# Transposes and value products of an attention stage in batches of two key block pairs, with the output transposes moved to another PSUM bank

## The chip, the cores and the metric

The kernel runs on one core of one Trainium2 chip. The metric is the device time of one execution in microseconds (us). The engines are TensorE (PE in the profile, with its weight loads as PEld), VectorE (DVE), ScalarE (ACT), GpSimd (POOL) and SyncE (SP, which only issues transfers here). TensorE writes to PSUM, which has eight banks of 128 partitions by 2 KB. The kernel is written in a tile framework: the code says what is computed on which engine, and a scheduler decides, when the program is built, in which order each engine gets its instructions; each engine then executes its list strictly in that order and waits on semaphores.

## The reference

Two layers on 2048 rows of 1024 features in float32. The first (a state space scan beside a convolution) is not touched. The second is sparse attention: an indexer scores all keys, each query keeps its best 256, and 16 heads (four per key head, 64 channels each) attend to the kept ones. Cut to what matters here:

```python
score = jnp.where((key_chunk <= c)[None, None, :], score, -jnp.inf)
_, idx = lax.top_k(score, ksel)                    # ksel = 256
...
logits = jnp.einsum("bqhgd,bqkhd->bqhgk", qb, kg) * scale
p = jax.nn.softmax(logits, axis=-1)
ob = jnp.einsum("bqhgk,bqkhd->bqhgd", p, vg)
...
out = (out * jax.nn.silu(z)) @ w_out
```

## The kernel before

The kernel does not gather keys. It finds each query's threshold by a binary search over the score's bits, writes an additive mask of 0 or a large negative number, and attends densely to all admissible keys with that mask.

**The attention stage.** Queries come in 16 tiles of 128 rows, in the order `ORDER = (3, 7, 4, 6, 5, 8, 2, 9, 1, 10, 11, 12, 0, 13, 14, 15)`. Tile i has `nb = i + 1` key blocks of 128 keys. A tile has four units (two pairs of key heads `kp` times two pairs of query heads `hp`), so there are 64 units; a unit has two key heads `e` and two query heads `h` of each. A unit goes through two functions:

- `weights` multiplies the stacked queries `qs` with the keys (`ps_s`, line 1117, two parts `kh` and `kl`); DVE adds the mask and finds the maximum (`lm` and `mx`, line 1121); ACT takes the exponential of `lm` in place (line 1132).
- `values` transposes the weights `lm` block by block on PE (`ps_pt`, line 1148, four 128x128 transposes for one pair of key blocks of one `e`, a "group"); a copy brings the group from PSUM to SBUF (`pT`, line 1153 on ACT; line 1151 on DVE for every other group of the two longest tiles); PE multiplies it with the values `v` (`ps_pv`, line 1155, two matmuls per group, each of which stands as two records in the trace). At the unit's end ACT copies the sum (`ov`, line 1159), PE transposes it back (`ps_ot`, line 1163, four transposes), and DVE multiplies it with the gate (`zt_a` and `avt`, line 62).

The loop emits `weights` of a unit, then `values` of the unit before, so the scheduler can fill gaps of the one with work of the other. The query stacks of the next two units (`ps_q`, line 772, copied by ACT as `qs`, line 774) come in between.

**PSUM in this stage.** `ps_s` has two buffers of two banks (`pq`). Pool `pt2` has three banks, which `ps_pt` and `ps_q` take in turn. Pool `pv` has one bank, which `ps_pv` and `ps_ot` share.

**The selection beside it.** The masks of tiles 12 to 15 are made during this stage by a generator (`select_mask`) that advances one step per 800 mask columns. A tile needs 34 counting passes over its scores. Tile 13 counts on ACT (line 994: a sign pass, then two instructions of one column each, lines 1002 and 1004); tiles 12, 14 and 15 count on DVE (line 977, with two small POOL instructions, line 69, between counts). Their buffers exist once, so tile 14 starts when tile 13 has finished, and tile 15 after 14. A mask must be complete before its tile's units.

Of the kernel before, what the change touches and what calls it, by code (L numbers as in the profile page):

```python
# [11 lines left out]
F32 = mybir.dt.float32  # L12
# [11 lines left out]
P = 128  # L24
# [18 lines left out]
class Tags:  # L43


    def __init__(self, *turns):
        self.turns, self.n = turns, {}
# [839 lines left out]
def index_scores(k, i, S, st, ip, tk, pi, identr, res):  # L887
# [10 lines left out]
    if res is not None:  # L898
        sc = res["sc"] = tk.tile([P, LATE * P], F32, tag="sc", name="sc", bufs=CHAINS + 1)
    split = res is not None  # L900
# [33 lines left out]
def all_mask(k, i, ip, width, mask_d):  # L934

    nc = k.nc
    nk = (i + 1) * P
    eq = ip.tile([P, width], BF16, tag="eq", name="eq", bufs=CHAINS)[:, 0:nk]
    nc.gpsimd.memset(eq, 0.0)
# [118 lines left out]
class Attend:  # L1058
# [3 lines left out]
    def __init__(self, k, S, kvt, pools, ident, identr, beside, pace):  # L1062
        self.k, self.S, self.kvt, self.ident, self.identr = k, S, kvt, ident, identr
        self.am, self.tm, self.qsp, self.ap, self.pp, self.ptp, self.pq, self.pt, self.pv_ = pools
        self.beside, self.pace, self.cols = beside, pace, 0
        self.masks = {}

    def load(self, i, kp):

# [66 lines left out]
    def values(self, t, hp, prob):  # L1136

        k, nc, ap_, ident = self.k, self.k.nc, self.ap, self.ident
        nb, kp = t["i"] + 1, t["kp"]
        np_ = P if nb > 1 else 64  # L1140
        po = self.pv_.tile([P, 2, 256], F32, tag="pv", name="ps_pv")
        for e in range(2):
            for b in range(0, nb, 2):
                n = min(2, nb - b)
                ps = self.pt.tile([P, 2, 2, 128], F32, tag="pt", name="ps_pt")
                for s in range(n):
                    for h in range(2):
                        nc.tensor.transpose(ps[:, s, h], prob[e][h][:, (b + s) * P:(b + s + 1) * P], ident)  # L1148
                pT = self.ptp.tile([P, 2, 256], F32, tag="pT", name="pT")
                if b % 4 == 2 and nb > 14:  # L1150
                    nc.vector.tensor_copy(pT[:, 0:n], ps[:, 0:n].rearrange("p s h q -> p s (h q)"))
                else:
                    nc.scalar.copy(pT[:, 0:n], ps[:, 0:n].rearrange("p s h q -> p s (h q)"))  # L1153
                for s in range(n):
                    nc.tensor.matmul(po[64 * s:64 * s + 64, e],  # L1155
                                     self.kvt[(b + s) // 8, kp][2][:, (b + s) % 8, e * 64:e * 64 + 64], pT[:, s],
                                     start=b == 0, stop=b + s >= nb - 2)
        ov = ap_.tile([P, 2, 256], F32, tag="ov", name="ov", bufs=2)
        nc.scalar.copy(ov[0:np_], po[0:np_])
        ps = self.pv_.tile([P, 2, 2, 128], F32, tag="pv", name="ps_ot")  # L1160
        for e in range(2):
            for h in range(2):
                nc.tensor.transpose(ps[:, e, h, 0:np_], ov[0:np_, e, h * P:h * P + P], ident[0:np_, 0:np_])  # L1163
        four = t["z"].rearrange("p (e g h c) -> p g e h c", e=2, g=2, h=2)[:, hp]
        rd = ap_.tile([P, 2, 2], F32, tag="rd", name="rd", bufs=4)
        nc.vector.reciprocal(rd, t["den"].rearrange("p (e g h) -> p g e h", e=2, g=2)[:, hp])
        zr = ap_.tile([P, 2, 2, 64], F32, tag="zr", name="zr", bufs=2)
        k.vtt(zr, four, rd[:, :, :, None].to_broadcast([P, 2, 2, 64]), ALU.mult, nc.gpsimd)
        k.vtt(four, ps[:, :, :, 0:64], zr, ALU.mult)
        if nb > 1:  # L1170
            u = ap_.tile([P, 2, 2, 64], F32, tag="avt", name="avt", bufs=2)
            k.vtt(u, ps[:, :, :, 64:128], zr, ALU.mult)
            k.vtt(four, four, u, ALU.add, nc.gpsimd)
        if hp == 1:
            nc.sync.dma_start(self.S["att"][t["rows"], 512 * t["kp"]:512 * t["kp"] + 512], t["z"])
# [2 lines left out]
ORDER = (3, 7, 4, 6, 5, 8, 2, 9, 1, 10, 11, 12, 0, 13, 14, 15)  # L1178
RATIO = 2
CHAINS = 3  # L1180
ON_ACT = (3, 5, 7, 9, 11, 13)
EARLY = 140
PACE = 800
# [4 lines left out]
def layer1(k, A, h1_d, S, ident, identr, vec):  # L1188
    nc, tc = k.nc, k.tc
    with ExitStack() as ctx:  # L1190
# [3 lines left out]
        with ExitStack() as c2:  # L1194
# [21 lines left out]
            def index(tiles):  # L1216

                todo, scoring, running, turn = list(tiles), None, [], 0
                while todo or scoring or running:
                    if scoring is None and todo and len(running) <= CHAINS:  # L1220
                        i = todo.pop(0)
# [5 lines left out]
                    if scoring and (not running or turn % RATIO == 0):  # L1227
                        if next(scoring[0], scoring) is scoring:
                            res, scoring = scoring[1], None
                            if res is not None:  # L1230
                                running.append(select_mask(k, res["i"], res["sc"], tk, LATE * P, CHAINS, S["mask"],
                                                       scalar=res["i"] in ON_ACT))
                    turn += 1
# [46 lines left out]
            def late():  # L1280
                for j in range(LATE, 16):
                    sc = tk.tile([P, L], F32, tag="sc", name="scr")
                    nc.sync.dma_start(sc[:, 0:(j + 1) * P], S["sc"][j, :, 0:(j + 1) * P])
                    yield from select_mask(k, j, sc, tk, L, 1, S["mask"], pace, scalar=j in ON_ACT)
                    done.add(j)
# [199 lines left out]
```

## Time and profile before

| what | value |
|---|---|
| median of 3 runs | 3014.05 us (3012.71 to 3017.12) |
| profiled execution | 3015.91 us, span 3014.1 us |
| mean granted clock of TensorE | 0.969 |
| attention stage in the trace | about 1799 to 2817 us of the span |
| transposes of the weights / value products | 2176 records each |
| after the stage (output projection) | 2817 to 3014 us |

A row of a group in the profile names line, engine, operation, what is written and read, count, then busy time and mean duration (ns), then the idle time of the engine just before. A row of the stretches gives, for each engine, the time in which it was busy, with the number of instructions, then the granted clock, the share of the transfer engines and GB/s. A row of the timeline gives start and duration in us, and how many instructions of one kind followed each other.

### The profile page before, as it was taken

To read this page: it belongs to the slowest core of one execution; us is meant where nothing else is said; L and a number is where in the kernel's file an instruction comes from. 1 tells how busy PE (TensorE), PEld (TensorE's weight loads), DVE (VectorE), ACT (ScalarE), POOL (GpSimd) and SP (SyncE) were. 2 spreads that over 40 slices of the span, in tenths; PEclk is the share of its full clock that TensorE was granted. 3 is DMA by queue.
4 is the path that set the end of the run, shared out by engine and by line. 5 is a ranking of instruction groups with operands and counts; after the bars stand their busy time and mean duration, and the time that the engine had idled before them with its cause. 6 is when DMAs were issued, how large, how long until landed. Compare 5 with 4: busy or idle time off the path is not lost. (4 is left out here: it accounts for less than half of the span.)

```text
span 3014.1 us, 47682 instructions
## 1 busy us (share of the span) xinstructions
PE 2753.4 (91%) x17488; PEld 2220.8 (74%) x17488; DVE 2072.8 (69%) x3735; ACT 1733.2 (58%) x3558; POOL 1105.6 (37%) x1517
## 2 busy tenths in 40 slices
PE   7789998799999999899889968999989999999998
PEld 5667786678999899899779946666655555666787
DVE  8899986995354556644897479734489997456444
ACT  4122332344243688888768957899965666655311
POOL 3946133732232697745774113321232121001000
PEclk9899999899999999999999979999999999999999
DMA  3254563346566323235322261111110101001332
GB/s 134 76 126 142 157 171 63 122 160 208 172 203 226 97 82 120 64 94 175 99 71 82 88 229 38 58 33 37 38 52 26 47 21 53 22 4 50 123 126 98
DMA packets 233385, 300.40 MB, mean 100 GB/s; under 512 B 14144, under 2 KB 171072, under 8 KB 233024
## 3 DMA queue, kind: packets, MB, share of 16 engines
q1 hardware_dynamic: 233152, 297.37, 31.4%
q8 instruction: 137, 2.24, 0.3%
q14 instruction: 96, 0.79, 0.1%
HBM read 194.16 MB, written 105.25 MB: 99 GB/s over the span
## 5 line engine op out<-in xcount | busy, mean ns | idle before, releaser
L114 POOL TENSOR_TENSOR wl<-wst,wh 128x512 fp32r<-128x512 f32 (+1 forms) x220 | 341.5, 1556 | 444.6 <-ACT wh L113 407.9
L121 PE MATMUL ps_tm<-wh,hb 128*128 128x256 f32 (+1 forms) x1536 | 439.3, 290 | 11.7 <-ACT ot L875 6.9
L122 PE MATMUL ps_tm<-wh,hb 128*128 128x256 f32 (+1 forms) x1536 | 444.4, 290 | 0.8 <-DVE hb L72 0.8
L123 PE MATMUL ps_tm<-wl,hb 128*128 128x256 f32 (+1 forms) x1536 | 439.9, 289 | 0.0
L1132 ACT ACTIVATE lm<-lm,mx 128x512 f32<-128x512 f32 (+15 forms) x256 | 309.1, 1209 | 135.0 <-DVE mx L1121 134.4
L1153 ACT COPY pT<-ps_pt 128x512 f32<-128x512 f32 (+1 forms) x512 | 273.6, 563 | 153.0 <-PE ps_pt L1148 127.0
L72 DVE SCALAR_TENSOR_TENSOR cvo<-hc,vec,cvo 128x1024 f32<-128x1024 f32 x240 | 356.0, 1514 | 0.8
L1121 DVE CUSTOM_DVE_ANT_0 lm<-ps_s,amb 128x1024 f32<-128x1024 f32 (+7 forms) x256 | 249.6, 985 | 152.2 <-PE ps_pt L1148 89.4
L1155 PE MATMUL ps_pv<-pT,v 128*64 128x256 f32 x2176 | 339.1, 399 | 14.6 <-DVE avt L62 8.6
L1148 PEld LDWEIGHTS ps_pt<-ident,lm 128*128 128x128 f32 x2176 | 240.1, 141 | 143.1 <-issue 125.0
L1148 PE MATMUL ps_pt<-ident,lm 128*128 128x128 f32 x2176 | 340.8, 282 | 1.8 <-ACT lm L1132 0.7
L1117 PE MATMUL ps_s<-kh,qs 128*128 128x512 f32 (+2 forms) x640 | 268.6, 421 | 48.7 <-DVE mx L1121 42.1
L121 PEld LDWEIGHTS ps_tm<-wh,hb 128*128 128x128 f32 x1536 | 296.2, 194 | 19.6 <-ACT ot L875 9.0
L69 POOL TENSOR_SCALAR sv<-sv 128x1 f32<-128x1 f32 x512 | 185.6, 363 | 321.6 <-DVE eq L977 282.9
L122 PEld LDWEIGHTS ps_tm<-wh,hb 128*128 128x128 f32 x1536 | 298.0, 194 | 6.0 <-DVE hb L72 1.5
L123 PEld LDWEIGHTS ps_tm<-wl,hb 128*128 128x128 f32 x1536 | 296.7, 194 | 4.3
L113 ACT CAST wh<-wst 128x512 fp32r<-128x512 f32 (+1 forms) x220 | 133.2, 609 | 283.2 <-DMA wst<-in_w_in 131.3
L121 PE MATMUL ps_p<-hh,wh 128*128 128x512 f32 x640 | 256.8, 404 | 18.9 <-ACT uT L520 16.5
L123 PE MATMUL ps_p<-hl,wh 128*128 128x512 f32 x640 | 256.9, 404 | 0.0
L122 PE MATMUL ps_p<-hh,wl 128*128 128x512 f32 x640 | 255.9, 400 | 0.0
L977 DVE TENSOR_SCALAR_CACHE_REDUCE eq<-klo,sv 128x384 bf16<-128x384 uint16 (+7 forms) x136 | 207.0, 1525 | 63.5 <-POOL sv L69 62.8
L977 DVE TENSOR_SCALAR_CACHE_REDUCE eq<-khi,sv 128x384 bf16<-128x384 uint16 (+7 forms) x136 | 206.8, 1525 | 48.7 <-POOL sv L69 47.4
(333 smaller groups left out, 6335.2 us busy)
## 6 DMA issues: line engine op xcount, KB each, us to landing
wst<-in_w_in SPq DMA_DIRECT2D x168, 256.0 KB, 2.9
zs_d<-zt SPq DMA_DIRECT2D x16, 512.0 KB, 3.3
zt<-zs_d SPq DMA_DIRECT2D x16, 512.0 KB, 4.4
ry<-rec_d SPq DMA_DIRECT2D x16, 512.0 KB, 4.2
xr<-in_x SPq DMA_DIRECT2D x16, 512.0 KB, 4.4
wst<-in_w_out SPq DMA_DIRECT2D x32, 256.0 KB, 3.4
h_d<-xr SPq DMA_DIRECT2D x16, 512.0 KB, 3.7
xt<-h_d SPq DMA_DIRECT2D x16, 512.0 KB, 5.7
```

What stands on the lines that cost most here:

```text
L72: self.nc.vector.scalar_tensor_tensor(out=out, in0=a, scalar=s, in1=b, op0=op0, op1=op1)
L114: nc.gpsimd.tensor_tensor(out=lo, in0=st, in1=hi.bitcast(F32), op=ALU.subtract)
L121: t.matmul(ps, a[0], b[0], start=start, stop=False)
L122: t.matmul(ps, a[1], b[0], start=False, stop=False)
L123: t.matmul(ps, a[0], b[1], start=False, stop=stop)
L977: op = nc.vector.tensor_scalar(out=eq, in0=src, scalar1=u, scalar2=0.0, op0=op, op1=ALU.add, accum_out=cnt)
L1117: nc.tensor.matmul(pss[e][:, cols], qs[e][:, 2 * hp + h], src[:, e, cols], start=part == 0, stop=part == 1)
L1121: self.pace[0] = nc.vector.tensor_tensor_reduce(out=prob[e][h][:, c:c + w], in0=pss[e][:, 0:w], in1=mb[:, c:c + w], scale=-0.125, scalar=( ...
L1132: nc.scalar.activation(lm, lm, AF.Exp, bias=mxs[e, h][:, nh - 1:nh], scale=-1.0, accum_out=t["den"][:, hd:hd + 1])
L1148: nc.tensor.transpose(ps[:, s, h], prob[e][h][:, (b + s) * P:(b + s + 1) * P], ident)
L1153: nc.scalar.copy(pT[:, 0:n], ps[:, 0:n].rearrange("p s h q -> p s (h q)"))
L1155: nc.tensor.matmul(po[64 * s:64 * s + 64, e], self.kvt[(b + s) // 8, kp][2][:, (b + s) % 8, e * 64:e * 64 + 64], pT[:, s], start=b == 0, s ...
```

## The change

The transposes and the value products of a unit are emitted in batches of two groups (`TURN = 2`). Two groups are transposed, then two more, then the products of the first two are made, and so on; the last batch has its products alone. `k.after` adds an edge for the scheduler without a semaphore: the first product of a batch stands behind the last transpose of the next batch, and the first transpose of a batch (also of the next unit's first batch, through `self.held`) stands behind the last product of the one before. The output transposes `ps_ot` take one of the three banks of `pt2` in place of the bank of `pv`. No arithmetic is added or removed.

```diff
-        for e in range(2):
-            for b in range(0, nb, 2):
-                n = min(2, nb - b)
-                ps = self.pt.tile([P, 2, 2, 128], F32, tag="pt", name="ps_pt")
+        def turned(group):
+            e, b = group
+            n = min(2, nb - b)
+            ps = self.pt.tile([P, 2, 2, 128], F32, tag="pt", name="ps_pt")
+            for s in range(n):
+                for h in range(2):
+                    op = nc.tensor.transpose(ps[:, s, h], prob[e][h][:, (b + s) * P:(b + s + 1) * P], ident)
+                    if self.held is not None:
+                        k.after(op, self.held)
+                        self.held = None
...
+            return e, b, n, pT, op
+        def weighted(groups, last):
+            for e, b, n, pT, _ in groups:
                 for s in range(n):
...
+                    op = nc.tensor.matmul(
+                        po[64 * s:64 * s + 64, e],
+                        self.kvt[(b + s) // 8, kp][2][:, (b + s) % 8, e * 64:e * 64 + 64], pT[:, s],
+                        start=b == 0, stop=b + s >= nb - 2)
+                    if last is not None:
+                        k.after(op, last)
+                        last = None
+            self.held = op
+        groups = [(e, b) for e in range(2) for b in range(0, nb, 2)]
+        before = None
+        for g in range(0, len(groups), TURN):
+            now = [turned(group) for group in groups[g:g + TURN]]
+            if before:
+                weighted(before, now[-1][4])
+            before = now
+        weighted(before, None)
...
-        ps = self.pv_.tile([P, 2, 2, 128], F32, tag="pv", name="ps_ot")
+        ps = self.pt.tile([P, 2, 2, 128], F32, tag="pt", name="ps_ot")
...
+TURN = 2
```

The scheduler rebuilds the order of all engines in the stage; ahead of the first transposes of the weights PE has the same instructions in the same order as before. Three places follow. Names and lines are those of the list above, with the new line numbers in the changed kernel (1150 transposes, 1165 products, 1158 and 1156 copies, 1183 `ov`, 1187 `ps_ot`).

On PE, near the end of a unit of tile 14, before:

```order
L1148 MATMUL ps_pt<-ident,lm 128x128 x8
L1155 MATMUL ps_pv<-pT,v_13488 64x256 x4
L1148 MATMUL ps_pt<-ident,lm 128x128 x4
L1155 MATMUL ps_pv<-pT,v_13488 64x256 x2
L1148 MATMUL ps_pt<-ident,lm 128x128 x4
L1155 MATMUL ps_pv<-pT,v_13488 64x256 x2
L1148 MATMUL ps_pt<-ident,lm 128x128 x4
L1155 MATMUL ps_pv<-pT,v_18929 64x256 x2
L1148 MATMUL ps_pt<-ident,lm 128x128 x2
L1155 MATMUL ps_pv<-pT,v_18929 64x256 x2
L772 MATMUL ps_q<-identr,tmq_27993 128x128 x4
```

The same part of the unit in the changed kernel:

```order
L1150 MATMUL ps_pt<-ident,lm 128x128 x8
L1165 MATMUL ps_pv<-pT,v_18929 64x256 x3
L1150 MATMUL ps_pt<-ident,lm 128x128 x8
L1165 MATMUL ps_pv<-pT,v_13488 64x256 x4
L1150 MATMUL ps_pt<-ident,lm 128x128 x8
L1165 MATMUL ps_pv<-pT,v_13488 64x256 x4
L1150 MATMUL ps_pt<-ident,lm 128x128 x6
L1165 MATMUL ps_pv<-pT,v_18929 64x256 x6
```

PE changes between the two kinds half as often here; runs of eight transposes and four products replace runs of four and two.

On ACT, within a unit of tile 8 (`eq` and `sv` belong to the selection of tile 13, lines 994 to 1006), before:

```order
L1006 ACTIVATE sv<-sv 128x1
L1153 COPY pT<-ps_pt 128x256
L1153 COPY pT<-ps_pt 128x512
L994 ACTIVATE eq,sv<-khi,sv 128x1792
L1153 COPY pT<-ps_pt 128x512 x2
L1132 ACTIVATE lm,den<-lm,mx 128x1152
L994 ACTIVATE eq,sv<-klo,sv 128x1792
```

The unit at the same place in the changed kernel:

```order
L994 ACTIVATE eq,sv<-klo,sv 128x1792
L1158 COPY pT<-ps_pt 128x512 x2
L1158 COPY pT<-ps_pt 128x256
L1002 ACTIVATE sv<-sv 128x1
L1132 ACTIVATE lm,den<-lm,mx 128x1152
L1004 ACTIVATE sv<-sv 128x1
L994 ACTIVATE eq,sv<-klo,sv 128x1792
L1183 COPY ov<-ps_pv 128x512
```

Before, this unit has the end of the first search (`khi`) and the start of the second (`klo`); in the changed kernel it is already some passes into the second. Counted over the order, the units of tiles 6, 5 and 8 hold 22 sign passes before and 33 in the changed kernel; the units of tiles 2 and 9 hold 11 before and none in the changed kernel.

On DVE, within a unit of tile 9, before:

```order
L62 TENSOR_TENSOR zt_a<-ps_ot,zr 128x2x128
L62 TENSOR_TENSOR avt<-ps_ot,zr 128x256
L1121 ISA lm,mx<-ps_s,amb 128x1024
L1121 ISA mx 128x1
L1121 ISA lm,mx<-ps_s,amb,mx 128x256
```

The same place in the changed kernel:

```order
L62 TENSOR_TENSOR zt_a<-ps_ot,zr 128x2x128
L62 TENSOR_TENSOR avt<-ps_ot,zr 128x256
L977 TENSOR_SCALAR eq,sv<-khi,sv 128x1920 x4
L1121 ISA lm,mx<-ps_s,amb 128x1024
L1121 ISA mx 128x1
```

The counts of tile 14 (line 977) now start in tile 9's units; before, DVE had none there. By tile, DVE counts before: tile 10 19, tile 11 15, tile 12 27, tile 0 6, tile 13 1. In the changed kernel: tile 9 18, tile 1 7, tile 10 10, tile 11 25, tile 12 8, and none after that.

More of the change, by code (lines that the diff above doesn't have):

```diff
@@ L1065, in __init__ @@
         self.beside, self.pace, self.cols = beside, pace, 0
-        self.masks = {}
+        self.masks, self.held = {}, None
     def load(self, i, kp):
@@ L1141, in values @@
         po = self.pv_.tile([P, 2, 256], F32, tag="pv", name="ps_pv")
-        for e in range(2):
-            for b in range(0, nb, 2):
-                n = min(2, nb - b)
-                ps = self.pt.tile([P, 2, 2, 128], F32, tag="pt", name="ps_pt")
-                for s in range(n):
[L1147 to L1157, printed above, removed]
+        def turned(group):
[8 more added lines that the diff above has]
+                        self.held = None
+            pT = self.ptp.tile([P, 2, 256], F32, tag="pT", name="pT")
+            if b % 4 == 2 and nb > 14:
+                nc.vector.tensor_copy(pT[:, 0:n], ps[:, 0:n].rearrange("p s h q -> p s (h q)"))
+            else:
+                nc.scalar.copy(pT[:, 0:n], ps[:, 0:n].rearrange("p s h q -> p s (h q)"))
+            return e, b, n, pT, op
```

## The prediction

> **What bounds the kernel now.** I read the page's shares first, then a table by stretch cut where tiles end (the `ps_ot` of a tile's last unit), then the PE timeline, and last the groups of the two engines that bind. From the page:
>
> ```profile
> span 3014.1 us, 47682 instructions
> PE 2753.4 (91%) x17488; PEld 2220.8 (74%) x17488; DVE 2072.8 (69%) x3735; ACT 1733.2 (58%) x3558; POOL 1105.6 (37%) x1517
> ```
>
> By shares PE is the bound everywhere. The stretches of the attention stage say otherwise (tiles 3, 7, 4; tiles 6, 5, 8; tiles 2, 9; tiles 1, 10, 11, 12; tile 0; tiles 13, 14, 15; then the output projection):
>
> ```profile
> 1799.00:1946.00 147.00, 134.32 (x870) 95.39 (x870) 137.19 (x244) 108.66 (x224) 51.36 (x106) 0.99 0.13 45
> 1946.00:2102.00 156.00, 148.65 (x989) 99.84 (x988) 61.75 (x165) 148.32 (x298) 29.05 (x49) 1.00 0.11 35
> 2102.00:2195.00 93.00, 89.02 (x604) 61.31 (x604) 47.00 (x124) 87.85 (x179) 20.14 (x33) 1.00 0.12 39
> 2195.00:2498.00 303.00, 275.83 (x1698) 172.02 (x1696) 281.19 (x448) 187.32 (x330) 78.19 (x189) 0.98 0.11 36
> 2498.00:2525.00 27.00, 22.72 (x111) 15.64 (x109) 22.02 (x54) 15.18 (x39) 7.50 (x15) 0.87 0.18 59
> 2525.00:2817.00 292.00, 289.63 (x1903) 190.90 (x1902) 161.80 (x284) 168.52 (x239) 34.26 (x40) 1.00 0.10 33
> 2817.00:3014.00 197.00, 188.15 (x856) 150.51 (x856) 94.09 (x273) 39.51 (x96) 3.14 (x2) 0.99 0.36 125
> ```
>
> The columns after the length are PE, PEld, DVE, ACT, POOL. In tiles 3, 7, 4 and again in 1 to 12, DVE is busy 93% of the time; in 6 to 9 ACT is, 94 to 95%; only in tiles 13 to 15 does PE run alone at 99%. The DVE and ACT peaks are the selection: tile 12's counts, then tile 13's on ACT, then 14's and 15's on DVE. PE's waits fit that, nearly all on DVE:
>
> ```profile
> PEld ps_s L1117 <- DVE mx L1121: 59.5, 80, 2.6
> PE ps_s L1117 <- DVE mx L1121: 37.3, 49, 2.4
> PE ps_pv L1155 <- DVE avt L62: 8.6, 13, 1.4
> ```
>
> So what PE saves lands in full in the last stretch only; elsewhere the sum must follow the engine that binds.
>
> **Part 1: fewer changes between transposes and products.** The price is in the timeline, four single groups and then one place where two groups already came together:
>
> ```profile
> 2318.19 0.65 PE L1155 MATMUL ps_pv<-pT,v 128*64 128x256 f32 x4
> 2318.78 0.66 PE L1148 MATMUL ps_pt<-ident,lm 128*128 128x128 f32 x4
> 2319.36 0.65 PE L1155 MATMUL ps_pv<-pT,v 128*64 128x256 f32 x4
> 2319.95 0.66 PE L1148 MATMUL ps_pt<-ident,lm 128*128 128x128 f32 x4
> ...
> 2657.48 1.09 PE L1148 MATMUL ps_pt<-ident,lm 128*128 128x128 f32 x8
> 2658.50 1.08 PE L1155 MATMUL ps_pv<-pT,v 128*64 128x256 f32 x8
> 2659.51 0.66 PE L1148 MATMUL ps_pt<-ident,lm 128*128 128x128 f32 x4
> ```
>
> Start to start, one group of products and one of transposes take 2319.36 - 2318.19 = 1.17 us, so two pairs 2.34; the two together take 2659.51 - 2657.48 = 2.03. A merged pair saves 0.31. The weight loads show why: they stand idle at each change.
>
> ```profile
> 2657.47 0.86 PEld L1148 LDWEIGHTS ps_pt<-ident,lm 128*128 128x128 f32 x8 [0.39 <-issue]
> 2658.50 0.63 PEld L1155 LDWEIGHTS ps_pv<-pT,v 128*64 128x64 f32 x8 [0.17 <-issue]
> ```
>
> The Trainium skill ("TensorE: Matmul & The Clock Gate", Part 3) says that PE pulls a weight load ahead of running matmuls where it targets another row group or the background buffer. By that rule changes would be free and this term zero; the two idle times disagree, at least for this pair of kinds.
>
> Where scores follow products, the cost of a change is not smaller:
>
> ```profile
> 2314.03 1.95 PE L1155 MATMUL ps_pv<-pT,v 128*64 128x256 f32 x16
> 2315.91 0.51 PE L1117 MATMUL ps_s<-kh,qs 128*128 128x512 f32 x1
> 2316.25 0.40 PE L1117 MATMUL ps_s<-kl,qs 128*128 128x512 f32 x1
> 2316.48 0.40 PE L1117 MATMUL ps_s<-kh,qs 128*128 128x512 f32 x1
> ```
>
> The first score matmul takes 0.34 us to the next start, the second 0.23: 0.11 more, against 0.06 of the first transpose after products. In the orders, runs of products fall from 401 to 313, because scores now split them (139 runs end at scores, 28 before). That is 88 x 0.31 = 27 us less, and 111 x (0.11 - 0.06) = 6 us more: PE has about 21 us less to do. Of it, tiles 13 to 15 have 132 - 97 = 35 runs: 10.9 less, 0.8 back, 10 us. The other 11 us lie where DVE or ACT bind.
>
> **Part 2: shorter distances.** `ps_ot` in a `pt2` bank removes the wait of products for `avt` (8.6 us above), but the third or fourth group of the next unit now waits for that same read of `avt`, with about as much PE work in between. I cost this move at nothing (-8.6 to +5). Products no longer overlap the next unit's transposes, so `ov` is waited for sooner: between the last product and `ps_ot` PE had 2.8 us of other work in the median, now 0.9, and 20 of 64 units have under 0.9 (counted in the orders, at the timeline's start-to-start times).
>
> ```profile
> L1159 ACT COPY ov<-ps_pv 128x512 f32<-128x512 f32 x12 | 7.1, 591 | 0.0
> ```
>
> A copy of 0.59 us, and any exponential ahead of it on ACT, must fit there. Bounds over 64 units: 0 (all covered) to 64 x 0.59 = 38 us; I take 8 in all, 3 of them in tiles 13 to 15, nearer the lower end as most units keep some scores there.
>
> **Part 3: the selection moves.** No DMA is added; the masks' DMAs on SP and POOL's small steps move with their counts. Tiles 6, 5, 8 get 33 sign passes in place of 22, and ACT is the bound there. One pass by rows of that stretch:
>
> ```profile
> L994 ACT ACTIVATE eq<-khi,sv 128x1792 bf16<-128x1792 uint16 x16 | 28.8, 1801 | 0.0
> L994 ACT ACTIVATE eq<-klo,sv 128x1792 bf16<-128x1792 uint16 x6 | 10.7, 1792 | 0.0
> L1002 ACT ACTIVATE sv<-sv 128x1 f32<-128x1 f32 x22 | 7.0, 317 | 0.0
> L1004 ACT ACTIVATE sv<-sv 128x1 f32<-128x1 f32 x21 | 6.4, 304 | 0.0
> L994 ACT ACTIVATION_READ_ACCUMULATOR eq<-khi,sv 128x1 f32 x16 | 3.2, 201 | 0.0
> ```
>
> 1.8 us alone, 1.80 + 0.20 + 0.32 + 0.30 = 2.62 with everything; ACT's neighbours overlap, so I take 2.2. Eleven more are 24 us (20 to 29). ACT's 148.3 us become 172, and at 98% busy the stretch takes 176 in place of 156: **+20**.
>
> Tiles 2 and 9 lose these 24 us on ACT, but DVE gets tile 13's end, tile 14's keys and 18 counts. The rows of the later stretch:
>
> ```profile
> L977 DVE TENSOR_SCALAR_CACHE_REDUCE eq<-khi,sv 128x1920 bf16<-128x1920 uint16 (+1 forms) x34 | 77.3, 2274 | 5.2 <-POOL sv L69 5.2
> L977 DVE TENSOR_SCALAR_CACHE_REDUCE eq<-klo,sv 128x1920 bf16<-128x1920 uint16 (+1 forms) x32 | 72.7, 2271 | 7.8 <-POOL sv L69 7.8
> L62 DVE TENSOR_TENSOR key<-key,scr 128x512 int32<-128x512 int32 (+1 forms) x8 | 5.6, 699 | 0.1
> L1048 DVE TENSOR_TENSOR_SCAN cum<-eq 128x1920 f16<-128x1920 bf16 x1 | 4.2, 4157 | 0.0
> ```
>
> 18 x 2.27 = 41, and some 12 for the rest: 47 + 53 = 100 us of DVE work in 93 us, most of it in tile 9. Between 95 (spread evenly) and 107 (tile 9 alone held by DVE): **+8**.
>
> Tiles 1, 10, 11, 12 lose 11 counts (25 us) and tile 13's end and tile 14's keys, and gain tile 15's end: about 30 us less, DVE 281 to 251. PE's 275.8 lose 30 runs: 9.3 less, 2 back, 269. Now PE would bind, at 96% busy 280; but tile 11 keeps 25 of 50 counts and is held by DVE, which holds the gain back. Between 269 and 303: **-22**. Tile 0 loses the last counts: 27 to about 21, **-6**. Tiles 13 to 15: -10 + 3 = -7, and tile 15's scan, which now ends earlier, -1: **-8**. Tiles 3, 7, 4 keep their counts and 38 runs of products: 0. The projection keeps its instructions: 0.
>
> **The sum.** +20 + 8 - 22 - 6 - 8 = -8 us against the profiled execution of 3015.9 (span 3014.1 and 1.8 around it), which is 1.9 above the median shown; taken off the median 3014.05, it gives 3006 us.
>
> **Rivals.** (a) PE's saving lands everywhere, since the buffers let DVE and ACT run a unit ahead and their loads even out: tiles 6 to 12 then cost +16, +2, -30, and with -6 and -10 the sum is -28: 2986 to 2994, I say 2990. For it: over the whole stage DVE is busy 711 of 1018 us (the sum of the first six stretches), so no engine but PE binds in total. Against it: in-order queues, with ACT already at 95% where it gets more. The Trainium skill ("Perfetto Trace Analysis", Identifying the Most-Contended Engine) would have one optimize the engine of highest occupancy first; by the profile's first rows that is PE (91%, and its weight loads at 74% are still above DVE's 69%), and its 21 us would come off: 2993. The same section adds that the most-contended engine may change over time and that mixing such regimes may help; the stretches above show such a change. (b) Slower: the selection, packed more densely, costs its full price and is not given back. With ACT at +24 and tile 9 at +14, and tiles 1 to 12 held at -17 by tile 11's counts and by the shorter distance of scores to DVE, then -3 and -6: +12, 3026. It decides from the point where tiles 1 to 12 give back less than about 20 us. For it: every wait on ACT in tiles 6 to 8 stands in front of scores on PE. (c) The batching does little: scores split the runs again and the order on the other engines happens to even out: 3014.
>
> **Chances.** My forecast 0.50, (a) 0.25, (b) 0.20, (c) 0.05. About 0.2% (6 us) is what a measurement of this kernel can tell from no change: faster is below 3008, slower above 3020. The forecast's own range is 2999 to 3015, so 0.30 of its 0.50 is faster, 0.19 the same, 0.01 slower; (a) is faster; (b) 0.02 the same, 0.18 slower; (c) the same. Together 0.55, 0.26, 0.19. The range leaves out half of (b)'s upper part and of (a)'s lower part: 2984 to 3025.
>
> **What would show it.** Right: in tiles 6, 5, 8 ACT over 96% busy and the stretch 15 to 25 us longer; L977 inside tile 9; the stretch to the end of tile 12 shorter by 15 us or more; tiles 13 to 15 in 282 to 287 us; PEld's idle before L1150 and L1165 down by about a fifth. Wrong: tiles 13 to 15 no shorter (then `ov` and the copies cost what the changes save), or tiles 6 to 8 as long as before (then ACT's queue had room).

## The result and the profile after

The changed kernel takes 3047.4 us (median, 3040.2 to 3054.5), beside 3015.6 us of the kernel before on the same chip: ratio 1.0102, 95% interval [1.0084, 1.0119]. It is slower by 1.0%; 3006 us was forecast, and the range ended at 3025. The page of its profile:

```profile
span 3052.8 us, 47706 instructions
PE 2754.9 (90%) x17488; PEld 2242.8 (73%) x17488; DVE 2073.7 (68%) x3735; ACT 1736.5 (57%) x3558; POOL 1115.0 (37%) x1517
```

Over the whole program the busy times are as before, so the 39 us between the two spans are idle time. The attention stage by the same stretches of tiles (3, 7, 4; 6, 5, 8; 2, 9; 1, 10, 11, 12; 0; 13, 14, 15; columns: length, then PE, PEld, DVE, ACT and POOL busy, the granted clock, DMA):

```profile
1813.00:1967.00 154.00, 138.39 (x850) 95.94 (x850) 138.22 (x244) 108.13 (x221) 50.63 (x106) 0.96 0.13 42
1967.00:2139.00 172.00, 150.15 (x981) 101.81 (x980) 62.97 (x166) 170.09 (x336) 28.31 (x48) 0.98 0.09 32
2139.00:2252.00 113.00, 97.24 (x613) 65.85 (x611) 102.31 (x187) 70.00 (x142) 31.98 (x73) 0.95 0.13 45
2252.00:2545.00 293.00, 267.94 (x1701) 180.00 (x1702) 241.37 (x409) 185.83 (x329) 63.60 (x151) 0.97 0.11 38
2545.00:2571.00 26.00, 24.69 (x135) 17.28 (x135) 17.94 (x45) 19.56 (x41) 7.43 (x13) 1.00 0.18 61
2571.00:2853.00 282.00, 278.32 (x1889) 192.81 (x1888) 149.14 (x267) 164.47 (x235) 32.88 (x39) 1.00 0.08 27
```

Against before the stretches are +7, +16, +20, -10, -1 and -10 us: some 22 us longer in sum. The other 17 us of the two spans lie ahead of the stage (it starts at 1813 instead of 1799, after the same instructions in the same order) and behind it; the repeat below shows that this part is chance.

What PE waited for in the stage (engine, waiting line, releaser: us in total, times, longest), changed kernel:

```profile
PE ps_s L1117 <- DVE mx L1121: 44.4, 48, 4.8
PE ps_ot L1187 <- ACT ov L1183: 11.3, 15, 1.7
PE ps_pt L1150 <- ACT pT L1158: 10.6, 14, 2.0
PE ps_pt L1150 <- ACT qs L774: 8.4, 11, 1.8
PE ps_pt L1150 <- DVE avt L62: 8.2, 9, 2.5
```

The kernel before has, in the same view:

```profile
PE ps_ot L1163 <- ACT ov L1159: 1.9, 3, 1.1
...
PE ps_pt L1148 <- ACT lm L1132: 0.7, 2, 0.5
...
PE ps_pt L1148 <- ACT qs L774: 0.5, 1, 0.5
```

The scores' wait in the first row is nearly as before: 4.8 of its 44.4 us stand ahead of the stage's first transpose, which leaves 39.6 against 37.3. The products' wait for `avt` (8.6 us) is gone, as the change meant. In its place transposes and output transposes wait 38.5 us, against 3.1 before. The end of tile 6's third unit shows three of the four waits (start, length, engine, line; in brackets the idle time and its releaser; the scores in between are of a later unit):

```profile
2001.75 1.94 PE L1165 MATMUL ps_pv<-pT,v 128*64 128x256 f32 x14
...
2003.79 1.77 ACT L994 ACTIVATE eq<-khi,sv 128x1792 bf16<-128x1792 uint16 x1
...
2004.31 0.28 PE L1117 MATMUL ps_s<-kl,qs 128*128 128x256 f32 x1
...
2005.57 0.56 ACT L1183 COPY ov<-ps_pv 128x512 f32<-128x512 f32 x1
...
2006.18 0.66 PE L1187 MATMUL ps_ot<-ident,ov 128*128 128x128 f32 x4 [1.59 <-ACT ov L1183]
2006.59 0.88 PE L772 MATMUL ps_q<-identr,tmq 128*128 128x128 f32 x8
...
2007.84 0.63 PE L1150 MATMUL ps_pt<-ident,lm 128*128 128x128 f32 x4 [0.36 <-DVE avt L62]
...
2008.07 1.04 ACT L774 CAST qs<-ps_q 128x512 fp32r<-128x512 f32 x2
...
2008.68 0.55 PE L1150 MATMUL ps_pt<-ident,lm 128*128 128x128 f32 x3 [0.22 <-ACT qs L774]
```

The last products and four scores are done by 2004.6; the copy of `ov` stands behind a sign pass on ACT and ends at 2006.1; PE runs nothing in between. Then the next unit's first transposes wait for `avt` and for `qs`, each of which empties one of the three shared banks. In the order of issue none of the 64 units has a group of the next unit ahead of its `ps_ot`; before, 3.7 groups stood there on average. Both tiles come from one pool in turn, so `ps_ot`, asked for first in the code, goes first, and all of the next unit's transposes queue behind it. The run with a late end, below, tests this reading.

### The profile page after: what moved, and what is told of

It is laid out like the page before. It is cut to its first block, busy times and chain, and to the rows that moved or that the text cites. A ratio compares the mean times of both kernels' runs of the same rounds, so it can differ in the third digit from the quotient of the medians.

```text
span 3052.8 us, 47706 instructions
## 1 busy us (share of the span) xinstructions
PE 2754.9 (90%) x17488; PEld 2242.8 (73%) x17488; DVE 2073.7 (68%) x3735; ACT 1736.5 (57%) x3558; POOL 1115.0 (37%) x1517
## 4 chain that ended last, share of the span: by engine, by line
PE 39%; DVE 15%; issue 7%; ACT 7%; POOL 7%; DMA 3%; SPq 0%; DVEq 0%; POOLq 0%; ACTq 0%
DVE eq L977 7%; PE ps_pv L1165 5%; PE ps_pt L1150 5%; PE ps_s L1117 5%; PE ps_tm L121 4%; PE ps_tm L123 4%; PE ps_tm L122 4%; POOL sv L69 3%; DVE lm L1121 2%; PE ps_o L122 2%; PE ps_o L121 2%; PE ps_o L123 2%; ACT eq L994 2%; ACT lm L1132 2%; POOL wl L114 1%
## 5 line engine op out<-in xcount | busy, mean ns | idle before, releaser
L114 POOL TENSOR_TENSOR wl<-wst,wh 128x512 fp32r<-128x512 f32 (+1 forms) x220 | 360.0, 1640 | 447.1 <-ACT wh L113 414.5
L1150 PE MATMUL ps_pt<-ident,lm 128*128 128x128 f32 x2176 | 318.4, 283 | 28.7 <-ACT pT L1158 10.6
L1150 PEld LDWEIGHTS ps_pt<-ident,lm 128*128 128x128 f32 x2176 | 246.4, 143 | 114.9 <-issue 65.8
L1165 PE MATMUL ps_pv<-pT,v 128*64 128x256 f32 x2176 | 320.9, 395 | 1.7 <-ACT pT L1158 1.2
L1117 PE MATMUL ps_s<-kh,qs 128*128 128x512 f32 (+2 forms) x640 | 272.7, 427 | 49.0 <-DVE mx L1121 44.4
L121 PEld LDWEIGHTS ps_tm<-wh,hb 128*128 128x128 f32 x1536 | 295.3, 193 | 21.1 <-ACT ot L875 10.6
L121 PE MATMUL ps_p<-hh,wh 128*128 128x512 f32 x640 | 259.5, 408 | 19.3 <-ACT uT L520 16.1
```

What stands on the lines that cost most here:

```text
L114: nc.gpsimd.tensor_tensor(out=lo, in0=st, in1=hi.bitcast(F32), op=ALU.subtract)
L121: t.matmul(ps, a[0], b[0], start=start, stop=False)
L1117: nc.tensor.matmul(pss[e][:, cols], qs[e][:, 2 * hp + h], src[:, e, cols], start=part == 0, stop=part == 1)
L1150: op = nc.tensor.transpose(ps[:, s, h], prob[e][h][:, (b + s) * P:(b + s + 1) * P], ident)
L1165: op = nc.tensor.matmul(po[64 * s:64 * s + 64, e], self.kvt[(b + s) // 8, kp][2][:, (b + s) % 8, e * 64:e * 64 + 64], pT[:, s], start=b == ...
```

## The experiments

Beside the times, the length of the stage in each profile (first transpose of weights to last `ps_ot`) is split in one way for all runs: every step from one PE start to the next beyond its usual length is a wait, the rest is work. This split is an estimate: another choice of the usual length moves it by some 10 us, and a matmul that ran longer at a lower clock counts partly as a wait. "PE busy" is the busy time in the profile's stretch rows, such longer matmuls included. "Runs" are runs of products between other matmuls. The ratio is to the kernel before on the same chip.

| kernel | us | to before | runs | stage | PE busy | PE work | waits |
|---|---|---|---|---|---|---|---|
| before | 3015.6 | | 401 | 1018 | 960 | 922 | 96 |
| changed | 3047.4 | 1.0102 | 313 | 1041 | 957 | 907 | 134 |
| batches alone | 3026.3 | 1.0037 | 331 | 1029 | 953 | 901 | 128 |
| bank alone | 3067.3 | 1.0174 | 476 | 1069 | 989 | 945 | 124 |
| changed, placed as before | 3041.2 | 1.0087 | 310 | 1042 | 957 | 905 | 137 |
| before, spread | 3002.6 | 0.9956 | 396 | 1004 | 952 | 917 | 86 |
| changed, late end | 3001.1 | 0.9949 | 354 | 1005 | 950 | 911 | 94 |

**Parts apart.** Theory T: the loss comes from where the selection's passes now stand. D: from a unit's end, where PE has no transposes left to fill the wait. B: the batches drain the pipeline themselves. Batches alone puts one line of the changed kernel back, bank alone changes that line in the kernel before; the third run repeats the changed kernel.

```
-        ps = self.pt.tile([P, 2, 2, 128], F32, tag="pt", name="ps_ot")
+        ps = self.pv_.tile([P, 2, 2, 128], F32, tag="pv", name="ps_ot")
```

> Batches of two groups with their edges as in the change, but ps_ot back in the bank of pv. In the built order the selection stands where it stood before (22 sign passes in tiles 6, 5, 8; 11 in tiles 2, 9; no count in tile 9), 2.4 groups of a later unit's transposes stand ahead of ps_ot (3.7 before, none in the change), and runs of products are 331 (401 before, 313 in the change). Both theories that blame the bank (T: the selection is placed worse; D: no transposes are left to fill the end of a unit) expect a gain over before: 70 runs x 0.31 us = 22 us less on TensorE, half of it covered by DVE and ACT, so 3000 to 3010 us against about 3015. Theory B (batching itself drains the pipeline at each unit's end, 64 units x 0.4 us) expects 3030 to 3045 us.

> The kernel before with nothing changed but ps_ot in a bank of pt2. The built order has the selection placed as in the change (32 sign passes in tiles 6, 5, 8, 20 counts in tile 9), no transposes ahead of ps_ot, and 476 runs of products. T and D expect the whole loss of the change and no saving from batches: 3050 to 3070 us (+32 of the change, +10 to +20 for the runs of products). B expects no loss: 3010 to 3020 us.

> The change itself, a second profile. In its first profile 12 us of 39 had already appeared ahead of the attention stage, where the orders of all engines are the same as before. If that is chance of the one execution, the part ahead of the stage comes back to within 4 us of before and the total lies at 3038 to 3050 us, with the stage 22 to 28 us longer than before. If it belongs to the program, the 12 us return.

Batches alone: 3026.3 us, ratio 1.0037 [1.0023, 1.0051]; bank alone 3067.3, 1.0174 [1.0160, 1.0188]; the changed kernel again 3042.4, 1.0095 [1.0081, 1.0108]. Neither part gains. Batches alone fall between what T and D (3000 to 3010) and what B (3030 to 3045) expected; bank alone is where T and D had it. The repeat starts its stage at 1797 and still loses as much: the stage's late start in the first profile is chance, its length (1044) is not. The profile of batches alone is of its slowest execution (3042.0 us); its stage starts at 1814, so the excess lies ahead of the stage. What PE waits for differs by part. Batches alone, then bank alone:

```profile
PE ps_s L1117 <- DVE mx L1121: 47.8, 46, 3.5
PE ps_pv L1165 <- DVE avt L62: 19.7, 28, 2.3
```

```profile
PE ps_ot L1163 <- ACT ov L1159: 11.1, 17, 2.9
PE ps_pv L1155 <- ACT pT L1153: 10.0, 16, 1.5
PE ps_pt L1148 <- DVE avt L62: 6.4, 7, 2.6
PE ps_pt L1148 <- ACT qs L774: 5.4, 10, 1.1
```

By the split the batches save 21 us of PE work (922 to 901; PE's busy time falls by 7), and they pay with longer waits, 19.7 us in place of 8.6 for the one bank of products and 47.8 in place of 37.3 at the scores. The bank move brings the waits at the unit's end, and in single groups it splits the runs as well (476). It is also the bank move that brings the selection forward: bank alone has 32 sign passes in tiles 6, 5, 8, batches alone 22 as before.

**Without the selection.** The four kernels with the searches of tiles 12 to 15 left out (their masks are a constant):

```
-                    yield from select_mask(k, j, sc, tk, L, 1, S["mask"], pace, scalar=j in ON_ACT)
+                    all_mask(k, j, tk, L, S["mask"])
+                    yield
```

> The kernel before without the searches of tiles 12 to 15 (their masks are written as constants, so those tiles' results are not the reference's). Only attention is left in the stage, and TensorE should bind: the stage falls from 1018 us to between 920 and 960 us, the total to about 2920 to 2960 us (steps made ahead of the stage go too). It is the reference for the next three.

> The change without the searches. Theory T (the loss is the selection's new place): without selection the change keeps its saving on TensorE, 95 runs of products fewer than in the run before this one, so 10 to 20 us faster than it. Theory D (no transposes left to fill the end of a unit): most of the loss stays, 5 to 25 us slower than it.

> Batches alone, ps_ot in the bank of pv, without the searches. T and D: 67 runs of products fewer, 10 to 20 us faster than the kernel before without searches. B (batching drains the pipeline): 10 to 25 us slower.

> The bank move alone, without the searches; 458 runs of products (397 in the kernel before without searches). T: 10 to 20 us slower than that kernel, for the 61 runs x 0.31 us only. D: 25 to 50 us slower, the runs and the ends of the units.

Before 2928.6 us, changed 2926.1, batches alone 2925.7, bank alone 2976.6. Against the first: -2.4, -2.9 and +48 us. So the change costs nothing where ACT and DVE have room, and 30 us where they don't. Without searches PE's busy time in the stage falls from 926.7 to 916.2 us, and its waits, up from some 8 us to 19, take that back. Bank alone loses nearly as much as with the selection (54): PE's busy time grows by 36 us of the stage's 51 (926.7 to 962.9), with 458 runs of products in place of 397, so most of its loss is not waits. PE's waits at transposes in the changed kernel without searches:

```profile
PE ps_ot L1187 <- ACT ov L1183: 3.3, 7, 0.8
PE ps_pt L1150 <- ACT qs L774: 2.0, 6, 0.3
PE ps_pt L1150 <- ACT pT L1158: 1.8, 5, 0.6
```

They are the same kinds, at a quarter of the length. The changed kernel and batches alone lie between what the theories expected (10 to 20 us faster, or 5 to 25 slower) and do not tell them apart; bank alone is where D had it, 25 to 50 us slower.

**Where the selection stands.** The steps are paced by a table of steps per tile in place of one per 800 columns; sign passes are also issued after the latest exponential. "Placed as before" puts the changed kernel's passes into the tiles where the kernel before has them; "spread" moves DVE's counts into tiles 10 to 14.

```
-                    while self.cols >= PACE:
-                        self.cols -= PACE
+                    while t["i"] in STEPS and self.cols >= 4096 * (t["i"] + 1) / STEPS[t["i"]]:
+                        self.cols -= 4096 * (t["i"] + 1) / STEPS[t["i"]]
...
-PACE = 800
+STEPS = {6: 21, 5: 18, 8: 27, 2: 12, 9: 26, 1: 6, 10: 69, 11: 67, 12: 82, 0: 18, 13: 20}
...
+STEPS = {6: 20, 5: 16, 8: 22, 2: 9, 9: 24, 1: 8, 10: 35, 11: 56, 12: 58, 0: 8, 13: 66, 14: 66}
```

> The changed kernel with the steps of the selection emitted evenly inside each tile by a table of counts (in place of one step per 800 columns), so that the passes of both engines stand in the tiles where they stood in the kernel before (sign passes on ScalarE 23 in tiles 6, 5 and 8 and 7 in tiles 2 and 9; counts on VectorE 9, 4, 21, 14, 29 in tiles 7, 4, 10, 11, 12 and 4 in tile 0). Theory T (the change loses because the selection stands in other tiles): tiles 6, 5, 8 fall from 172 to 150-158 us, tiles 2 and 9 from 113 to 93-100, tiles 1, 10, 11, 12 rise to about 300, in all 3010 to 3022 us. Theory D (the loss is the waits at the shared banks, whatever stands beside them): it stays at 3036 to 3048 us.

> The kernel before with the same table idea, but the counts on VectorE spread over tiles 10 to 14 (6, 20, 12, 3 in tile 0, 22, 5) instead of tiles 10 to 12 and ScalarE's passes where they were. If VectorE's counts are what makes tiles 10, 11 and 12 longer than in the kernel without searches (302 against 258 us) and tiles 13 and 14 have room for them, tiles 1, 10, 11, 12 fall to 270-285, tiles 13 to 15 stay within 5 of 292, in all 2985 to 3000 us. If a pass costs the same wherever it stands, or tiles 13 to 15 get as much longer, 3010 to 3025 us.

> The batches alone (output transposes in the products' banks, as before) with the same spread of the selection. Theory T: with the selection out of the way what is left is the gain that the runs without searches showed (batches 3 us faster than the kernel before), so 0 to 8 us under the spread kernel with groups in turn. Theory D: batches wait more beside any selection, 8 to 20 us over it, as with the selection as the 800 columns place it (13 us over).

> The changed kernel (batches and output transposes in the weights' transposes' banks) with the same spread table. Theory T: it stands within 8 us of the spread kernel without the change, as it did without searches (2 us faster). Theory D: 15 to 35 us over it, as with the selection as the 800 columns place it (30 us over).

Changed, placed as before: 3041.2 us, 1.0087 [1.0072, 1.0101]. That is the time of theory D (3036 to 3048), and T falls: the passes stand nearly where they stood (26 sign passes in tiles 6, 5, 8, 22 before and 33 in the changed kernel; 7 in tiles 2 and 9, 11 before) and the loss stays. Tiles 6, 5, 8 of that run:

```profile
1955.00:2124.00 169.00, 149.26 (x991) 102.28 (x990) 61.85 (x165) 156.18 (x310) 28.37 (x48) 0.99 0.09 32
```

ACT has 156 us of work in 169 us, and the stretch is still 13 us longer than before. So ACT's amount of work there does not set the length; 11.7 us of PE's waits there are still for `ov`, `pT` and `qs`. The spread gives 3002.6 before (0.9956 [0.9942, 0.9971]), 3013.9 with batches alone (0.9989 [0.9979, 1.0000]) and 3040.0 with the whole change (1.0078 [1.0063, 1.0092]): it gains 13 us by itself, tiles 1, 10, 11 and 12 fall from 303 to 280 us, and the change costs 37 us on top, a little over D's 15 to 35. The spread gains for the kernel before and does not help the change; batches alone cost 11 us on top, as D expected.

**Which engine's queue.** The passes keep their number and order, but one engine's run over 64 columns instead of a row (the masks of tile 13, or of 12, 14 and 15, then come from a part of the row; the second cut also scales the count's threshold).

```
+        n = 64 if pace and pace[0] else nk
-        nc.scalar.activation(eq, src, AF.Sign, bias=nu, accum_out=cnt)
+        nc.scalar.activation(eq[:, 0:n], src[:, 0:n], AF.Sign, bias=nu, accum_out=cnt)
```

> The kernel before, with ScalarE's sign passes of the selection, from the attention stage on, over 64 columns instead of a whole row (tile 13's mask is then not the reference's; the passes' number and order of issue stay). Only to be compared with the same cut in the changed kernel. About 33 passes of 1.8 us are taken off ScalarE in the stage: 2975 to 3000 us.

> The changed kernel with the same cut. Theory A (the change loses because the copies of a unit's end stand behind sign passes on ScalarE): the difference to the kernel before with the cut falls from 30 to between 0 and 12 us. Theory V (because the emptying of the shared banks stands behind counts on VectorE): it stays at 20 to 30.

> The kernel before with VectorE's counts of the selection, from the stage on, over 64 columns (the masks of tiles 12, 14 and 15 are then not the reference's). Some 95 passes of 2.2 us are taken off VectorE, which binds tiles 10 to 12: 2935 to 2975 us. Only to be compared with the same cut in the changed kernel.

> The changed kernel with the same cut. Theory V: the difference to the kernel before with the cut falls from 30 to between -5 and 12 us. Theory A: it stays at 18 to 30 us. If both engines carry a part, both cuts leave about half, 10 to 18.

Thin on ACT: before 3005.2, changed 3013.2, a loss of 8 us. Thin on DVE: 2972.0 and 2990.0, a loss of 18. Uncut it is about 30 (29 in the repeat, 32 in the result). So some 22 us of the loss hang on ACT's sign passes and 12 on DVE's counts; by the stage's length alone, where the loss falls from 23 us to 6 and to 16, it is 16 and 7. Together that is about the whole. The loss of 8 is as theory A expected, that of 18 lies on the border between A and a part for both engines; the thin sign passes gained less in the kernel before than expected (3005 us, not 2975 to 3000). PE's waits at transposes in the changed kernel, thin on ACT, then thin on DVE:

```profile
PE ps_pt L1151 <- DVE avt L62: 10.9, 12, 2.4
PE ps_ot L1188 <- ACT ov L1184: 7.9, 16, 1.3
PE ps_pt L1151 <- ACT qs L774: 4.4, 8, 1.2
PE ps_pt L1151 <- ACT pT L1159: 3.8, 8, 0.8
```

```profile
PE ps_ot L1191 <- ACT ov L1187: 9.9, 11, 1.7
PE ps_pt L1154 <- ACT pT L1162: 8.9, 11, 2.0
PE ps_pt L1154 <- ACT qs L774: 7.7, 11, 1.8
PE ps_pt L1154 <- DVE avt L62: 4.9, 6, 1.2
```

The three waits on ACT sum to 30.3 us uncut and to 16.1 with thin sign passes, while the wait on `avt` rises from 8.2 to 10.9. With thin counts it falls to 4.9, which is only a part of what the counts cost.

**The order at a unit's end.** The changed kernel with one thing moved: the output transposes and what reads them are written after the first batch of the next unit's transposes. Banks and batches stay.

```
         for g in range(0, len(groups), TURN):
             now = [turned(group) for group in groups[g:g + TURN]]
+            if po is None:
+                self.finish()
+                po = self.pv_.tile([P, 2, 256], F32, tag="pv", name="ps_pv")
...
         nc.scalar.copy(ov[0:np_], po[0:np_])
+        self.last = t, hp, ov
+
+    def finish(self):
...
         ps = self.pt.tile([P, 2, 2, 128], F32, tag="pt", name="ps_ot")
```

> The changed kernel with the output transposes of a unit, and what reads them, written after the first batch of the next unit's transposes. In the order of issue 1.7 groups of the next unit then stand between the last product and the output's transposes (none in the changed kernel, 3.7 before); the banks stay shared; TensorE has 354 runs of products instead of 313, +13 us at 0.31 each. Theory O (the order at a unit's end is what exposes TensorE to the two queues): its waits at transposes and output transposes fall from 57 to 15-30 us, so 3018 to 3030 us in all. Theory B (the sharing of the banks as such): they stay over 45 us, and it ends at 3040 to 3055 us.

3001.1 us, ratio 0.9949 [0.9932, 0.9966]: 41 us under the changed kernel's repeat, more than theory O expected (3018 to 3030), and faster than both kernels. Its waits at transposes, which sum to 7.8 us with two smaller ones, against 38.5:

```profile
PE ps_pt L1149 <- DVE avt L62: 2.4, 4, 1.0
PE ps_ot L1200 <- ACT ov L1185: 2.2, 5, 0.7
PE ps_pt L1149 <- ACT pT L1157: 1.7, 6, 0.6
```

and the end of the same unit of tile 6, first ACT, then PE:

```profile
1976.88 1.83 ACT L994 ACTIVATE eq<-khi,sv 128x1792 bf16<-128x1792 uint16 x1
...
1979.59 0.61 ACT L1185 COPY ov<-ps_pv 128x512 f32<-128x512 f32 x1
```

```profile
1976.02 0.65 PE L1164 MATMUL ps_pv<-pT,v 128*64 128x256 f32 x2
1976.59 1.09 PE L1149 MATMUL ps_pt<-ident,lm 128*128 128x128 f32 x8
1977.44 0.48 PE L1117 MATMUL ps_s<-kh,qs 128*128 128x512 f32 x1
...
1980.25 0.65 PE L1200 MATMUL ps_ot<-ident,ov 128*128 128x128 f32 x4
```

Its copy of `ov` starts 2.9 us after the end of the last products (1.9 in the changed kernel), behind a sign pass and an exponential, yet `ps_ot` waits for nothing: a batch of the next unit's transposes and twelve scores lie in between. The banks are shared as in the changed kernel, so the order at the unit's end, not the sharing, was the loss. This order also lets the selection fall back near its old tiles (24 sign passes in tiles 6, 5, 8), but the run "placed as before" showed that this alone gives about 1 us against the repeat. It ends 25 us under batches alone too; how it takes away the cost of the batches was not separated.

**Searches on other engines.** Tile 15's search on ACT and tile 13's on DVE, with a table that spreads both; once on the kernel before, once on batches alone.

```
-ON_ACT = (3, 5, 7, 9, 11, 13)
+ON_ACT = (3, 5, 7, 9, 11, 15)
```

> The kernel before with the search of tile 15 on ScalarE and that of tile 13 on VectorE, and the steps spread by a table: VectorE's counts of tiles 13 and 14 over tiles 7 to 12 (11, 12, 7, 12, 11, 3, 2, 3, 9, 10, 11), ScalarE's passes in tiles 13, 14 and 15 (12, 16, 4). Tiles 6, 5, 8, 2 and 9 lose ScalarE's passes (249 us before, 231 for tiles 6 to 8 and 2, 9 without searches), tiles 1, 10, 11 and 12 get 33 counts instead of 60 (302 us before, 258 without), tiles 13 to 15 get 32 passes (292 before, 285 without): 2965 to 2995 us if the queues are what the searches cost, 3005 to 3020 if a pass costs the same anywhere.

> The batches alone (output transposes in the products' banks) with the same swap and table: 329 runs of products against 388, some 18 us less on TensorE. If the batches cost their waits only beside a full queue: 3 to 15 us under the swap without batches. If they drain what they save in any case: within 3 us of it or over it.

3016.9 us (0.9998 [0.9987, 1.0009]) and 3050.4 us (1.0106 [1.0088, 1.0125]): neither gains. The first time is the one expected if a pass costs the same anywhere, but the trace shows another reason. The fifteen tiles ahead of tile 15 take 880 us instead of 922, but tile 15's mask is finished too late and its scores wait:

```profile
PE ps_s L1119 <- DVE mx L1123: 29.5, 2, 29.2
```

Tile 15 takes 141 us instead of 96, and that eats the gain; the table put the last passes too late. With batches alone the kernel is 33 us slower than the swap without them, and 19 of these are the products' wait for `avt`, the read that empties their only bank (27.2 us instead of 8.3). What batches with `ps_ot` in that bank cost depends on where the searches stand: -3 us without them, 11 with the spread, 13 as paced, 33 here, though DVE's busy time in the stage is about the same in the last three (711, 715 and 704 us). A late end together with a spread of the selection was not run.

## Why the prediction was wrong

**The step that failed: "I cost this move at nothing (-8.6 to +5)"** in part 2. Added to the batches, the bank move costs 16 us (3026.3 to 3042.4), and 26 with the selection spread (3013.9 to 3040.0). I saw that "products no longer overlap the next unit's transposes" and priced one consequence, `ov`, at 8 us: 11.3 in the profile, near. I put the read of `avt` at "the third or fourth group of the next unit", "with about as much PE work in between". But no group of the next unit goes ahead of `ps_ot` any more, so the whole start of the next unit stands behind it. There its first two groups wait 8.4 us for `qs`, its first four 8.2 for `avt` (5.1 of it at the first two; in 30 of 64 units two query stacks come first), and the fourth most of the 10.6 for `pT`: 27 us, against 1 before, for which the range had 5 at most.

**A second step had no term: what the batches cost by themselves.** The sum has only their saving, but alone they cost 13 us on the same chip (3013.1 to 3026.3). Their saving comes in tiles 13 to 15 (286 us instead of 292); tiles 1, 10, 11 and 12, beside DVE's counts, take 325 instead of 303. The scores there wait 31.5 us for `mx` instead of 17.0 and the products 9.5 for `avt` instead of 4.2. Why the scores wait longer stays open.

**Part 1, PE work: right in kind, too large.** PE does 15 us less in the stage by the split of the table, against 21 forecast, and its busy time falls by 3.4 us (960.2 to 956.7), since matmuls ran longer (see the last section). Without searches it falls by 10.5 for 95 runs fewer, where 0.31 us each would be 29, less what the scores take back. Tiles 13 to 15 take 282 us (282 to 287 forecast, -8 forecast, -10 measured). PEld's idle time by "issue" before the transposes and products falls by a third, a fifth was named. Before, then changed (busy, mean ns | idle by releasers):

```profile
L1148 PEld LDWEIGHTS ps_pt<-ident,lm 128*128 128x128 f32 x2176 | 240.1, 141 | 143.1 <-issue 125.0 <-ACT pT L1153 4.0 <-ACT lm L1132 2.8
L1155 PEld LDWEIGHTS ps_pv<-pT,v 128*64 128x64 f32 x2176 | 132.9, 136 | 118.5 <-issue 49.0 <-ACT pT L1153 15.4 <-PE ps_pt L1148 5.6
```

```profile
L1150 PEld LDWEIGHTS ps_pt<-ident,lm 128*128 128x128 f32 x2174 | 246.0, 143 | 114.6 <-issue 65.8 <-ACT pT L1158 16.1 <-ACT qs L774 12.5
L1165 PEld LDWEIGHTS ps_pv<-pT,v 128*64 128x64 f32 x2176 | 137.2, 136 | 105.3 <-issue 52.5 <-ACT pT L1158 7.6 <-ACT lm L1132 3.2
```

The transposes' loads gain it; the products' loads don't (49.0 to 52.5). Part of it goes to copies: before the transposes the idle time ended by `pT` rises from 4.0 to 16.1 us, and 12.5 for `qs` are new, while before the products that for `pT` falls from 15.4 to 7.6.

**Part 3, tiles 6, 5, 8: +20 forecast, +16 measured, for a wrong reason.** ACT is indeed 99% busy. But with its passes nearly back in their old places 13 of the 16 us stay. In the changed kernel that stretch's waits for `pT`, `ov` and `qs` sum to 16.8 us. A full engine looked like the bound; it was the queue in front of the copies. The prediction's table did not single ACT out either: in that stretch PE is busy for 148.65 of the 156 us, ACT for 148.32.

**The other stretches, forecast and measured:** tiles 2, 9: +8, +20; tiles 1, 10, 11, 12: -22, -10; tiles 3, 7, 4: 0, +7; tile 0: -6, -1. With the passes placed as before, the first three are +7, +1 and +8. The selection's move therefore gave about 13 us away in tiles 2 and 9 and got 11 back in tiles 1 to 12, near nothing in sum. What is left there, +8 in tiles 3, 7, 4, +13 in tiles 6, 5, 8 and +7 in tiles 2 and 9, is not the selection's place. DVE's counts in tile 9 were as forecast (43.7 us of line 977 in that tile, 41 by the prediction's count); that the rest of the tile would not fit beside them was not.

**The rivals.** (b) had the sign and its test (tiles 1 to 12 give back less than 20 us: 10), but its time, 3026, was 21 us short, and its cause, the selection packed more densely, fell with the run "placed as before". (a), that the buffers even things out, did not come in this kernel; another order, the late end, ends 15 us under the kernel before, where (a) had 24.

## What to carry over

Before a tile is moved into a pool that another producer takes in turn, write down what stands on the waiting engine between the last product and the tile's first use, before and after: a pool's turn is also an order, and it can put a whole unit behind one copy. Time saved on the busiest engine is not yet time saved: some 10 to 15 us less matmul work gave 2 us without searches, came with a loss of 30 in the changed kernel and with a gain of 15 with the late end. What differed was what else PE could run while a copy stood in another engine's queue. In this kernel the remedy was to write the dependent tail of a unit after the first independent work of the next one.

## What was not expected of the hardware

The stretch ahead of the attention stage, with the same instructions in the same order, ends between 1793.7 and 1813.8 us in the profiles of the kernels with searches, so one profile's span can't be compared with another's to better than some 20 us; the stage's own length repeats better (1040.9 and 1044.4 in the changed kernel's two profiles).

In tiles 2 and 9 of the changed kernel PE waited more, its granted clock was lower and its matmuls were longer: the clock went from 1.00 to 0.95 and the mean of one PE instruction from 89.02/604 = 147 ns to 97.24/613 = 159 ns, 8 of the stretch's 20 us. Without the selection the changed kernel has 1.00 and 145 ns there (88.93 us for 613). Stretches cut finer show when it happened; PE had waited 2.28 us, up to 2191.9, for `mx`:

```profile
2189.50:2193.10 3.60, 1.32 (x8) 0.96 (x7) 3.60 (x5) 0.58 (x1) 0.54 (x2) 1.00 0.00 0
2193.10:2196.50 3.40, 3.40 (x18) 3.01 (x16) 3.40 (x7) 2.07 (x4) 1.93 (x5) 0.50 0.00 0
```

For 3.4 us the clock, the third number from the end, is halved. Over the stage the halved stretches add up to some 46 us in the changed kernel and 19 before, so at half speed up to 13 us of the loss may be slower matmuls that follow the waits. It is not a matter of the sum of the waits: with the bank alone PE waits about as long, some 80 us in both, with some 26 us of halved clock. No run changes the clock and nothing else.
